# State space columns of a two-block transformer kernel computed in f32 ahead of the shift vector, with the first merge turned to tokens

## Chip, cores and metric

The kernel runs on one core of one Trainium2 chip, as one launch for the whole network. The metric is the device time of one execution in microseconds; the runs shown are three executions on the chip. "PE" is the matmul engine (TensorE), "PEld" its weight load, "DVE" VectorE, "ACT" ScalarE, "POOL" GpSimd, "SP" the engine that issues most DMAs.

## What is computed

Two blocks on 256 tokens of width 2048, batch 1, all in float32. The change touches the first block and the conditioning ahead of it:

```python
mod = silu(c) @ w_ada + b_ada                 # w_ada 2048 x 12288
sh1, sc1, g1, sh2, sc2, g2 = split(mod, 6)
h = rms_norm(x, norm_mix_g) * (1.0 + sc1) + sh1
proj = h @ w_in                               # w_in 2048 x 8192
u, q, k, v, ga, gb = split(proj, ...)         # widths 1024 x4, 2048 x2
y_ssm = s5_branch(u, ...)                     # 64 groups of 16 channels, 64 states
y_att = moba_attention(q, k, v, rel_bias)     # 256 tokens are one block: causal, with a bias
merged = (sigmoid(ga) * (y_ssm @ w_proj_ssm) + sigmoid(gb) * (y_att @ w_proj_attn))
x = x + g1 * (merged @ w_out)
h2 = rms_norm(x, norm_mlp_g) * (1.0 + sc2) + sh2
x = x + g2 * (square(relu(h2 @ w_ff1)) @ w_ff2)
```

The second block (another attention, a recurrence, and an expert layer whose rows are gathered by index) follows; the change edits nothing in it.

## The kernel before

Activations lie on chip transposed: channel on the partition, 256 tokens along the row, so a 2048-wide tensor is 16 chunks of 128 x 256. Weights stream from DRAM in pieces of 1 MB (four chunks of 128 rows, 512 columns). `gemm` (L528) takes one piece at a time. `piece` splits it into a high part (ACT, tile `wh`) and a rest (DVE, tile `wl`), both in the fast fp32r type; the activations are split likewise when they are written (class `HL`). A piece then costs three passes: high times high, high times rest, rest times high. There are two kinds. In kind "A" the weight chunk is the stationary operand and 256 token columns move, so that the output `ga` comes out by channel: 16 matmuls of 256 columns per pass. In kind "B" the tokens are stationary and 512 weight columns move; the output `gb` comes out by token: 8 matmuls of 512 columns per pass.

Order. While the flag `pinned` is set (the prologue), PE, DVE and ACT keep the order in which the program names their work. After that the scheduler of the tile framework places instructions by its own estimates. Between pieces `bg` (called at the end of each part of a piece) hands out credits: `dve` of them let background generators go on (the state space scan, attention, bias set-up), `rate` of them let the stream of conditioning loads go on (`stream`, the later columns of w_ada). TUNE["d1"] is the first of the two in block 1, TUNE["r1"] the second. A `drain` runs a generator to its end, and `need` forces the stream on until a vector is there.

Buffers. 1 MB tiles come from three rings: W with four buffers, H and L with two each. In the prologue all eight serve as landing buffers for the loads (`rot_tile`), in a gemm W holds raw pieces and H and L the split ones.

Prologue, three parts:

- The scale vector (1 + sc1). Sixteen loads of 1 MB of w_ada go through PE with the conditioning vector as stationary operand (tile `aw`, output `adap`; `ada_pe` L261). Beside them `x_in` (L885) transposes x (PE, tile `xt`), copies it to `xT` (DVE) and computes 1/rms of each token (`rstd`); `ssm_prep` (L614) discretizes the state space parameters (transposed in tile `ptp`, copied to `prm`), builds a table of powers of the recurrence (`ssm_table`, L691, tile `tab`: doubling steps of six DVE operations and four small ones each), and the block-diagonal operands (`ssm_blocks`, L722, tiles `bd`, `cd`, transposed on PE as `pb`, `pc`). The state space matrices b_re, b_im are loaded by `load_src` (L315) in runs of 64 bytes into `ssrc`.
- The shift vector sh1, again sixteen loads through PE (loop L921). In the gaps DVE scales x^T by 1/rms and by the scale (`mod_scale`), one chunk per load.
- `mod_shift` adds the shift and splits h into its two fp32r parts, `h1h` and `h1l`.

Main part of block 1, all by `gemm`: u (L953), then q, k, v, gb with a tanh for the sigmoid, w_proj_attn, ga, w_glu, w_proj_ssm with the merge (`ev_mrg`, L1070), w_out. u, q, k, ga, gb, w_glu, w_proj_attn and w_proj_ssm are kind "A", v and w_out kind "B". The scan on u (`ssm`, L761) and attention run as background work.

Of the kernel before, what the change touches and what calls it, by code (L numbers as in the profile page):

```python
# [79 lines left out]
def tile_kernel(ctx: ExitStack, tc: tile.TileContext, I, out):  # L80
# [354 lines left out]

    def modulate(xp, rstd, a, sh, hl, keep=None, then=None):
        n, ts, lag = 2 * len(xp), {}, 3
        for i in range(n + lag):
            if i < n:
                ts[i] = scr([P, L], "mt") if keep is None else keep[i // 8][:, i % 8, :]  # L440
                mod_scale(xp, rstd, a, i, ts[i])
            c = i - lag
            if c >= 0:
                mod_shift(ts[c], sh, c, hl)
                if c in (3, 7) and then is not None:
                    then()
# [167 lines left out]
    def ssm_prep():  # L614
# [268 lines left out]
    r0 = []  # L883

    def x_in():  # L885
        st = tiny([P, 2], "xst")
# [11 lines left out]
        r = rsqrt_of(st, 1.0 / D, 2)
        yield 1.0
        rs = scr([P, L], "rstd")  # L900
        S.copy(rs, spread([r[:, t:t + 1] for t in range(2)], pmisc([P, L], "rows")))
        r0.append(rs)
        yield 0.1
# [928 lines left out]
```

## Time and profile before

| | us |
|---|---|
| median of 3 runs | 3307.53 (3304.88 to 3307.8) |
| the profiled execution, device time | 3305.08 |
| its span in the trace | 3303.3 |
| PE busy | 2944.7 (89%) |
| DVE busy | 2265.6 (69%) |
| ACT busy | 951.7 (29%) |
| POOL busy | 829.6 (25%) |
| DMA moved | 1068.90 MB, mean 324 GB/s |

The span runs from the first to the last instruction of the profiled execution; the device time of the same execution is 1.8 us longer. Busy shares are means over stages with different limits, so they say little about one stage. The stages are: 0 to 75 us the scale vector, 75 to 115 the shift vector, 115 to 786 the gemms of block 1 up to w_out, 786 to 1500 its feed-forward, 1500 to 3303 the second block.

### The profile page before, as it was taken

The page shows a single profiled execution, that of the slowest core. Times are in us where ns is not written, and L with a number is a line of the kernel's source. Part 1 is how long each engine was busy: PE and PEld are TensorE (multiplying, and loading weights), DVE is VectorE, ACT ScalarE, POOL GpSimd, SP SyncE. Part 2 cuts the span into 40 slices and gives each one's busy share as a digit, 9 for nine tenths or more (in the row PEclk, how much of TensorE's full clock was granted, in tenths as well). Part 3 has the DMA queues.
Part 4 walks back from the last instruction along what each step waited for, and adds up shares of the span by engine and source line. Part 5 has one row for each costly group of instructions (what it writes and reads, how often), then busy time and mean ns, then how long its engine had stood idle before and what let it go on. Part 6 is the DMA issues. An engine that isn't in the chain of part 4 may idle for free.

```text
span 3303.3 us, 39102 instructions
## 1 busy us (share of the span) xinstructions
PE 2944.7 (89%) x15580; PEld 2136.2 (65%) x15580; DVE 2265.6 (69%) x3360; ACT 951.7 (29%) x1271; POOL 829.6 (25%) x540
## 2 busy tenths in 40 slices
PE   5899999999999999999999997979777768777777
PEld 2687889988999888898999886544322223222222
DVE  6688779777789888877776647555655565555542
ACT  1333433444433333345346631111111101111000
POOL 1000000000000000000000005656666666666663
PEclk8899999999999999999999998989999989999999
DMA  9876677877899999985783459999999999999998
GB/s 364 306 238 217 203 238 240 318 275 242 295 332 326 325 336 313 336 282 170 262 275 116 146 178 372 420 418 420 421 422 421 421 422 421 422 421 421 421 421 344
DMA packets 280459, 1068.90 MB, mean 324 GB/s; under 512 B 27380, under 2 KB 35991, under 8 KB 189525
## 3 DMA queue, kind: packets, MB, share of 16 engines
q1 hardware_dynamic: 202306, 524.35, 46.0%
q0 software_dynamic: 74752, 538.26, 39.2%
q10 hardware_dynamic: 3220, 3.81, 0.4%
q8 instruction: 122, 2.00, 0.2%
q14 instruction: 59, 0.48, 0.0%
HBM read 1064.24 MB, written 2.11 MB: 323 GB/s over the span
## 4 chain that ended last, share of the span: by engine, by line
PE 59%; DMA 31%; DVE 6%; issue 2%; ACT 1%; POOL 1%; SPq 0%; ACTq 0%; DVEq 0%; POOLq 0%
PE ga L94 30%; DMA dn<-in_peer_down_dram,eid 26%; PE gb L94 16%; PE pe L94 4%; DMA up<-in_peer_up_dram,eid 3%; DVE dn L94 2%; PE adap L94 2%; DMA aw<-in_w_ada_dram 2%; PE xt L94 1%; DMA aw<-in_ada_w_dram 1%; PE wqp L94 1%; PE o L94 1%; PE yp L94 1%; DVE wl L94 1%; PE bu L94 1%
## 5 line engine op out<-in xcount | busy, mean ns | idle before, releaser
L1698 POOL DMA_INDIRECT dn<-in_peer_down_dram,eid x256 | 517.2, 2020 | 2244.9 <-DVE g L94 1948.7
L94 PE MATMUL pe<-up,cdg 128*128 128x512 f32 x1792 | 824.4, 609 | 254.3 <-DMA up<-in_peer_up_dram,eid 203.6
L94 DVE SCALAR_TENSOR_TENSOR dn<-dn,htok 128x2048 f32<-128x2048 f32 x256 | 585.7, 2290 | 486.7 <-DMA dn<-in_peer_down_dram,eid 486.5
L94 PEld LDWEIGHTS pe<-up,cdg 128*128 128x128 f32 x1792 | 333.3, 193 | 735.7 <-issue 511.8
L94 ACT ACTIVATE wh<-w 128x2048 fp32r<-128x2048 f32 (+1 forms) x284 | 538.9, 1897 | 862.1 <-PE ga L94 476.2
L94 DVE TENSOR_TENSOR wl<-w,wh 128x2048 fp32r<-128x2048 f32 (+1 forms) x284 | 643.3, 2266 | 169.4 <-ACT wh L94 119.8
L1698 POOL DMA_INDIRECT up<-in_peer_up_dram,eid x224 | 260.9, 1165 | 139.2 <-issue 51.5
L94 DVE SCALAR_TENSOR_TENSOR acc<-aw,cT,acc 128x2048 f32<-128x2048 f32 x105 | 246.8, 2350 | 64.4 <-DMA aw<-in_ada_w_dram 46.3
L94 PE MATMUL ga<-h2h,wh 128*128 128x256 f32 x1024 | 249.0, 283 | 0.0
L94 PE MATMUL ga<-h2l,wh 128*128 128x256 f32 x1024 | 248.7, 283 | 0.0
L94 PE MATMUL ga<-h1h,wh 128*128 128x256 f32 x896 | 222.2, 287 | 0.0
L94 PE MATMUL ga<-h1l,wh 128*128 128x256 f32 x896 | 219.3, 284 | 0.0
L94 PE MATMUL gb<-wh,ah 128*128 128x512 f32 x512 | 199.6, 390 | 0.0
L94 PE MATMUL gb<-wh,al 128*128 128x512 f32 x512 | 199.4, 390 | 0.0
L94 PEld LDWEIGHTS ga<-h2h,wh 128*128 128x128 f32 x1024 | 196.5, 192 | 1.9 <-issue 1.7
L94 PEld LDWEIGHTS ga<-h2l,wh 128*128 128x128 f32 x1024 | 196.5, 192 | 0.2
L94 PEld LDWEIGHTS ga<-h1h,wh 128*128 128x128 f32 x896 | 172.0, 192 | 15.5 <-issue 12.1
L94 ACT ACTIVATE cdg<-ca,cf 128x128 f32<-128x128 f32 x224 | 77.0, 393 | 354.7 <-PE pe L94 347.4
L94 PEld LDWEIGHTS ga<-h1l,wh 128*128 128x128 f32 x896 | 172.2, 192 | 1.3 <-issue 1.2
L94 PE MATMUL ga<-h2h,wl 128*128 128x256 f32 x1024 | 134.1, 283 | 0.0
L94 PE MATMUL ga<-h3h,wh 128*128 128x256 f32 x528 | 132.1, 288 | 0.0
L94 PE MATMUL ga<-h3l,wh 128*128 128x256 f32 x528 | 132.0, 288 | 0.0
(437 smaller groups left out, 4287.6 us busy)
## 6 DMA issues: line engine op xcount, KB each, us to landing
w<-in_w_ff_dram SPq DMA_DIRECT2D x128, 1024.0 KB, 6.5
w<-in_w_in_dram SPq DMA_DIRECT2D x100, 1024.0 KB, 5.5
aw<-in_w_ada_dram SPq DMA_DIRECT2D x96, 1024.0 KB, 6.9
aw<-in_ada_w_dram SPq DMA_DIRECT2D x96, 1024.0 KB, 7.0
w<-in_w_out_dram SPq DMA_DIRECT2D x32, 1024.0 KB, 5.2
wq<-in_peer_wq_dram SPq DMA_DIRECT2D x16, 1024.0 KB, 10.2
w<-in_w_proj_attn_dram SPq DMA_DIRECT2D x8, 1024.0 KB, 5.2
w<-in_w_proj_ssm_dram SPq DMA_DIRECT2D x8, 1024.0 KB, 5.2
```

Source lines behind the costliest of these rows:

```text
L94: r = f(*a, **k)
L1698: r = G.indirect_dma_start(out=rows_, out_offset=None, in_=table, in_offset=bass.IndirectOffsetOnAxis(ap=idx, axis=0))
```

## The change

What it does, in the order of the program:

1. `x_in` computes 1/rms first and multiplies it in where x^T is copied from PSUM, so that xT holds the normalized input.
2. b_re and b_im are loaded as two contiguous blocks (tile `raw`, 64 groups x 1024 values) and brought into place by 64 small f32 matmuls against columns of the identity (tile `sb`: `raw` stationary, 32 columns moving) and two ACT copies.
3. The first two of the four tables of powers (`ssm_table(0)`, `ssm_table(1)`) are built in the prologue (before: the first there ahead of the scale vector, two more behind it; the rest by the scan itself); the block-diagonal operands (`ssm_blocks`, now in `ssm_mats`) and the attention bias come behind it as background work.
4. The u columns leave the gemms. While the shift vector loads, u is computed in plain f32 from the input scaled by (1 + sc1) alone: eight 1 MB loads of w_in (tile `wu`), 128 matmuls of 128 x 256 (tile `up`). Of the shift vector's own sixteen loads PE takes four, DVE accumulates the other twelve (`ada_both`, tile `acc`).
5. `u_shift`, ahead of the other loads in the stream: the u columns of w_in are loaded once more (8 MB), the shift vector is multiplied with them on PE (32 columns stationary), and the result is added to uT as a bias per channel. Then the rest of the preparation is drained and the scan started.
6. q is the first gemm (stream rate 1.25 instead of 0.65).
7. gb, w_proj_attn, ga and w_proj_ssm (16, 8, 16 and 8 pieces) become kind "B": gates and merge by token. The merged rows are turned back by 32 transposes on PE (tile `mt`) before they are split for w_out.
8. TUNE["d1"] goes from 3.6 to 4.0.

The diff, cut to its core:

```diff
-TUNE = {"r1": 0.65, "d1": 3.6, ...
+TUNE = {"r1": 0.65, "d1": 4.0, ...
...
+    raw = unit([64, 2, 1024], "raw")
+    for k, n in enumerate(("ssm_b_re", "ssm_b_im")):
+        SY.dma_start(raw[:, k, :], I[n][0].rearrange("g n q -> g (n q)"))
...
-        for k, n in enumerate(("ssm_b_re", "ssm_b_im")):
-            SY.dma_start(src[:, k, :].rearrange("p (t q) -> p t q", t=32),
-                        I[n][0].rearrange("(t g) n q -> (g n) t q", g=2))
...
+        par = ident[0:64, 0:64].rearrange("p (t g) -> p g t", g=2)
+        for k in range(2):
+            ps = pmisc([P, 32, 16], "sb")
+            rv = raw[:, k, :].rearrange("g (n q) -> g n q", q=16)
+            for q in range(16):
+                for g in range(2):
+                    T.matmul(ps[64 * g:64 * g + 64, :, q], rv[:, :, q], par[:, g, :], start=True, stop=True,
+                             skip_group_check=True)
+            S.copy(src[:, k, :], ps.rearrange("p t q -> p (t q)"))
+            yield 0.1
         yield from ssm_table(0)
+        yield from ssm_table(1)
+    def ssm_mats():
         for pp in range(2):
             bc = unit([P, 2, 2, 512], "bct")
             for k in range(2):
                 cp2 = 2 * pp + k
                 bct[cp2] = [bc[:, k, i, :].rearrange("p (r c m) -> p r c m", r=2, c=2) for i in range(2)]
                 yield from ssm_blocks(cp2, src)
-        for cp2 in range(1, 3):
-            yield from ssm_table(cp2)
...
+        r = rsqrt_of(st, 1.0 / D, 2)
+        rs = scr([P, L], "rstd")
+        S.copy(rs, spread([r[:, t:t + 1] for t in range(2)], pmisc([P, L], "rows")))
+        yield 1.0
...
-            V.tensor_copy(xp[c2], pt)
+            V.tensor_mul(xp[c2], pt, rs.unsqueeze(1).to_broadcast([P, 2, L]))
...
+    def ada_both(blk, j, g):
+        dest = const([P, 16], "mod")
+        ps = pacc_([P, 512], "adap")
+        acc = unit([P, D], "acc")
+        for kc in range(NC):
+            wt = rot_tile("aw")
+            SY.dma_start(wt, adaw[blk][kc * P:(kc + 1) * P, j * D:(j + 1) * D])
+            if kc == 0:
+                V.tensor_scalar(acc, wt, ccol[blk][:, 0:1], None, op0=OP.mult)
+            elif kc % 4 < 3:
+                V.scalar_tensor_tensor(acc, wt, ccol[blk][:, kc:kc + 1], acc, op0=OP.mult, op1=OP.add)
+            for l, r in [(crep[:, kc, :], wt)] * (kc % 4 == 3) + [(ones[:, 0:32], acc)] * (kc == NC - 1):
+                for q in range(4):
+                    T.matmul(ps[32 * q:32 * q + 32, :], l, r[:, 512 * q:512 * q + 512], start=(kc == 3),
+                             stop=(r is acc), skip_group_check=True)
+            yield 0.0
+        ada_fin(blk, j, ps, dest, g)
...
+    def u_load(nb, k):
+        wt = rot_tile("wu").rearrange("p (c n) -> p c n", c=4)
+        SY.dma_start(wt, w_in[4 * k * P:(4 * k + 4) * P, nb * 512:nb * 512 + 512]
+                     .rearrange("(c p) n -> p c n", p=P))
+        return wt
+    for i in range(8):
+        nb, k = divmod(i, 4)
+        wt = u_load(nb, k)
+        if k == 0:
+            ups = [pmisc([P, 2, L], "up") for _ in range(2)]
+        for _ in range(2):
+            next(g_sh1)
+            bg(0.5, 0)
+        if i == 7:
+            for _ in g_sh1:
+                pass
+        for kk in range(4):
+            c = 4 * k + kk
+            if nb == 0:
+                xx, a_ = xp[c // 2][:, c % 2, :], mods[(1, 1)][:, c:c + 1]
+                if kk % 2:
+                    S.activation(xx, xx, AF.Copy, scale=a_)
+                else:
+                    V.tensor_scalar(xx, xx, a_, None, op0=OP.mult)
+            for j in range(4):
+                T.matmul(ups[j // 2][:, j % 2, :], wt[:, kk, j * P:(j + 1) * P], xp[c // 2][:, c % 2, :],
+                         start=(c == 0 and j % 2 == 0), stop=(c == NC - 1), skip_group_check=True)
+        if nb == 0 and k == 3:
+            for j in range(2):
+                S.copy(uT[:, 2 * j:2 * j + 2, :], ups[j])
     h = HL(16, "h1")
-    for i, _ in enumerate(ada_pe(1, 0, None, crep, pacc_, True)):
-        if i < NC:
-            mod_scale(xp, rstd, mods[(1, 1)], i, xp[i // 2][:, i % 2, :])
-        bg(2.3, 0)
     pre = []
     for c in range(NC):
         mod_shift(xp[c // 2][:, c % 2, :], mods[(1, 0)], c, h)
         if c in (3, 7):
-            pre.append(piece(I["w_in"][0], c - 3, 4, 0, 512))
+            pre.append(piece(w_in, c - 3, 4, 1024, 512))
+        if c == 3:
+            for j in range(2):
+                S.copy(uT[:, 4 + 2 * j:6 + 2 * j, :], ups[j])
     pinned[0] = False
+    g_mats = start(ssm_mats())
+    start(moba_bias())
+    g_scan = []
+    def u_shift():
+        rep = scr([P, NC, 32], "shrep")
+        V.tensor_copy(rep, mods[(1, 0)].unsqueeze(2).to_broadcast([P, NC, 32]))
+        ps = pmisc([P, 512], "adap")
+        for k in range(8):
+            wt = wp.tile([P, 2, 1024], F32, name=nm("wu"), tag="W")
+            SY.dma_start(wt, w_in[2 * k * P:(2 * k + 2) * P, 0:1024].rearrange("(c p) n -> p c n", p=P))
+            for c in range(2):
+                for q in range(2):
+                    T.matmul(ps[32 * (2 * c + q):32 * (2 * c + q) + 32, :], rep[:, 2 * k + c, :],
+                             wt[:, c, 512 * q:512 * q + 512], start=(k == 0), stop=(k == 7),
+                             skip_group_check=True)
+            yield 0.0
+        ev = scr([P, 512], "adae")
+        S.copy(ev, ps)
+        pt = pmisc([P, 4, P], "adat")
+        for b in range(4):
+            T.transpose(pt[:, b, :], ev[:, 128 * b:128 * b + 128], ident)
+        two = tiny([P, 2, 2, 4], "us")
+        V.tensor_copy(two, pt.rearrange("p b (c q r) -> p c q b r", c=2, q=2)[:, :, :, :, 0])
+        b8 = tiny([P, 8], "ub")
+        V.tensor_add(b8.rearrange("p (q b) -> p q b", q=2), two[:, 0], two[:, 1])
+        for c in range(8):
+            S.activation(uT[:, c, :], uT[:, c, :], AF.Identity, bias=b8[:, c:c + 1])
+        drain(g_ssm, g_mats)
+        g_scan.append(start(ssm()))
+        yield 0.0
...
-    uT = unit([P, 8, L], "uT")
-    for nb in range(2):
-        gemm(w_in, NC, nb * 512, [("A", 512, store_pairs([uT], 4 * nb))], h, rate=TUNE["r1"], dve=TUNE["d1"], pre=pre if nb == 0 else ())
-    drain(g_ssm)
-    g_ssm = start(ssm())
...
-        gemm(w_in, NC, 1024 + nb * 512, [("A", 512, store_pairs([qT], 4 * nb, scale=SCALE))], h, rate=TUNE["r1"], dve=TUNE["d1"])
+        gemm(w_in, NC, 1024 + nb * 512, [("A", 512, store_pairs([qT], 4 * nb, scale=SCALE))], h, rate=1.25,
+             dve=TUNE["d1"], pre=pre if nb == 0 else ())
+        if nb == 0:
+            start(moba_flip())
+    drain(g_us)
...
+    def tanh_rows(dst, nb):
+        def ev(t, b):
+            S.activation(dst[t][:, 512 * nb:512 * nb + 512], b, AF.Tanh, scale=0.5)
+        return ev
+    sgb = [unit([P, D], "sgb") for _ in range(2)]
     for nb in range(4):
-        gemm(w_in, NC, 6144 + nb * 512, [("A", 512, store_pairs(sgb, 4 * nb, AF.Tanh, 0.5))], h, rate=TUNE["r1"], dve=TUNE["d1"])
+        gemm(w_in, NC, 6144 + nb * 512, [("B", 512, tanh_rows(sgb, nb))], h, rate=TUNE["r1"], dve=TUNE["d1"])
...
-        gemm(wpa, 8, nb * 512, [("A", 512, ev_m2)], oh, rate=TUNE["r1"], dve=TUNE["d1"])
-    sga = [unit([P, 8, L], "sga") for _ in range(2)]
...
-        gemm(w_in, NC, 4096 + nb * 512, [("A", 512, store_pairs(sga, 4 * nb, AF.Tanh, 0.5))], h, rate=TUNE["r1"], dve=TUNE["d1"])
+        gemm(w_in, NC, 4096 + nb * 512, [("B", 512, tanh_rows(sga, nb))], h, rate=TUNE["r1"], dve=TUNE["d1"])
...
-        def ev_mrg(i, b, nb=nb):
-            c = 4 * nb + 2 * i
-            m = scr([P, 2, L], "mrg")
-            V.scalar_tensor_tensor(m, sga[c // 8][:, c % 8:c % 8 + 2, :], 1.0, b, op0=OP.add, op1=OP.mult)
-            V.tensor_add(m, m, sgb[c // 8][:, c % 8:c % 8 + 2, :])
-            mh.put2(c, m)
-        gemm(I["w_proj_ssm"][0], 8, nb * 512, [("A", 512, ev_mrg)], yh, rate=TUNE["r1"], dve=TUNE["d1"])
+        def ev_mrg(t, b, nb=nb):
+            sl = slice(512 * nb, 512 * nb + 512)
+            m = sga[t][:, sl]
+            V.scalar_tensor_tensor(m, m, 1.0, b, op0=OP.add, op1=OP.mult)
+            V.tensor_add(m, m, sgb[t][:, sl])
+            if t == 0:
+                return
+            for c in (4 * nb, 4 * nb + 2):
+                pt = pmisc([P, 2, L], "mt")
+                for k in range(2):
+                    for tt in range(2):
+                        T.transpose(pt[:, k, tt * P:(tt + 1) * P], sga[tt][:, (c + k) * P:(c + k + 1) * P], ident)
+                mh.put2(c, pt)
+        gemm(I["w_proj_ssm"][0], 8, nb * 512, [("B", 512, ev_mrg)], yh, rate=TUNE["r1"], dve=TUNE["d1"])
```

In the listings below a row is one instruction (or a run of like ones, the last "x" number) in the order in which its engine gets it: operation, output tile, input tiles, shape. A number behind a name counts allocations and differs between the two kernels.

DVE of the kernel before, around the end of the scale vector (`tab` and `el` the second table, `mod_141` the scale vector, `xT` the input):

```order
L94 TENSOR_SCALAR cd_623<-ssrc_135,ca_81 128x2x64 x4
L94 MEMSET tab_634 128x8 x2
...
L94 COPY el_637<-e_142_648 128x8
L94 TENSOR_TENSOR mod_141<-adat_655,colT_103 128x16
L94 SCALAR_TENSOR_TENSOR mod_141<-mod_141,colT_103 128x16
L94 TENSOR_TENSOR ta_662<-tab_634,el_637 128x8x2
L94 TENSOR_TENSOR tab_634<-tab_634,el_637 128x8x2
```

The same place with the change (`tab_535` the second table, `mod_144` the scale vector, `acc_689` the accumulator of the shift vector):

```order
L94 COPY el_538<-e_131_662 128x8
L94 TENSOR_TENSOR mod_144<-adat_675,colT_103 128x16
L94 SCALAR_TENSOR_TENSOR mod_144<-mod_144,colT_103 128x16
L94 TENSOR_SCALAR acc_689<-aw_690,cT_94 128x2048
L94 SCALAR_TENSOR_TENSOR acc_689<-aw_693,cT_94,acc_689 128x2048
L94 TENSOR_SCALAR xT_142<-xT_142,mod_144 128x256 x2
L94 SCALAR_TENSOR_TENSOR acc_689<-aw_718,cT_94,acc_689 128x2048
L94 TENSOR_SCALAR xT_142<-xT_142,mod_144 128x256 x2
```

Before, the block-diagonal operands stand ahead of the scale vector and nearly all of the second table behind it; now the whole second table stands ahead of it, the operands far behind, and two accumulations of the shift vector come before the first scaled chunk.

PE with the change, where the small matmuls for b_re and b_im stand (`ptp` the parameters, `xt` the transposes of x, `sb` the new matmuls):

```order
L94 MATMUL ptp_294<-ca_81,ws_133 128x32 x5
...
L94 MATMUL xt_301<-ca_81,xtok_86 128x128
L94 MATMUL sb_307<-ca_81,raw_130 64x32 x32
L94 MATMUL xt_341<-ca_81,xtok_85 128x128
...
L94 MATMUL adap_145<-aw_347,crep_96 32x512 x4
L94 MATMUL sb_353<-ca_81,raw_130 64x32 x32
L94 MATMUL xt_387<-ca_81,xtok_85 128x128
```

Before, the transposes `xt` and the loads `adap` follow each other there without the 64 `sb` matmuls; the transposes of x behind them, and the DVE operations that need those, now come after.

PE with the change, at the end of the shift vector (`up` the u columns, `adap_688` the shift vector, `ga_976` the first matmul of q):

```order
L94 MATMUL adap_688<-aw_890,crep_96 32x512 x4
L94 MATMUL adap_688<-acc_689,ones_87 32x512 x4
L94 MATMUL adat_902<-ca_81,adae_900 128x128 x4
L94 MATMUL up_810<-xT_143,wu_885 128x256 x2
...
L94 MATMUL rr_1009<-hot_98,rb_100 8x512
L94 MATMUL pb_1016<-ca_81,bd_995 128x128 x4
L94 MATMUL ga_976<-h1h_924,wh_938 128x256
```

Before, `adat` is followed by the gemm of u; now the gemm of q stands there, behind the last of the 128 f32 matmuls and the first of the operands that left the prologue.

## Rows read from the trace of the kernel before

**Rows 1.** Stages: length, busy us (instructions) of PE, PEld, DVE, ACT, POOL; clock, DMA share, GB/s.

```profile
75.00:115.00 40.00, 28.55 (x153) 6.72 (x153) 35.38 (x161) 7.16 (x13) 0.00 (x0) 0.76 0.98 392
115.00:437.00 322.00, 322.00 (x2347) 271.07 (x2348) 230.90 (x411) 116.37 (x122) 0.00 (x0) 1.00 0.69 226
437.00:575.00 138.00, 137.96 (x1102) 124.27 (x1102) 131.04 (x266) 46.04 (x33) 0.00 (x0) 1.00 0.72 243
575.00:786.00 211.00, 211.00 (x1416) 193.30 (x1416) 163.71 (x117) 99.01 (x103) 0.00 (x0) 1.00 0.82 288
786.00:1500.00 714.00, 708.56 (x4635) 645.70 (x4634) 587.86 (x421) 287.11 (x235) 0.00 (x0) 1.00 0.89 310
```

**Rows 2.** Timeline of PE, first gemm of block 1: start, length, operation, last number the records.

```profile
114.88 0.58 PE L94 MATMUL ga<-h1h,wh 128*128 128x256 f32 x1
116.33 0.35 PE L94 MATMUL ga<-h1h,wh 128*128 128x256 f32 x1
```

**Rows 3.** Timeline of PE in the feed-forward: last pass of two pieces of each kind.

```profile
805.06 2.08 PE L94 MATMUL ga<-h2h,wl 128*128 128x256 f32 x16
810.82 2.08 PE L94 MATMUL ga<-h2h,wl 128*128 128x256 f32 x16
...
1083.25 1.98 PE L94 MATMUL gb<-wl,ah 128*128 128x512 f32 x8
1088.69 1.98 PE L94 MATMUL gb<-wl,ah 128*128 128x512 f32 x8
```

**Rows 4.** Timeline of PE: one conditioning load, a run of transposes, a run of f32 matmuls.

```profile
165.57 1.06 PE L94 MATMUL adap<-aw,crep 128*32 128x512 f32 x8
...
1992.85 1.91 PE L94 MATMUL tok<-ca,hf 128*128 128x128 f32 x16
1994.60 13.98 PE L94 MATMUL wqp<-hf,wq 128*128 128x256 f32 x64
```

**Rows 5.** Timeline of DVE in the prologue; in brackets idle time and what ended it.

```profile
34.60 0.30 DVE L94 COPY prm<-ptp 128x160 f32<-128x160 f32 x1
...
36.17 0.08 DVE L94 MEMSET tab<- 128x8 f32 x2
...
38.28 0.69 DVE L94 COPY xT<-xt 128x512 f32<-128x512 f32 x1 [0.65 <-PE xt L94]
38.89 0.17 DVE L94 TENSOR_TENSOR ta<-tab,el 128x16 f32<-128x16 f32 x1
...
40.09 0.67 DVE L94 COPY rrs<-rr 8x512 f32<-8x512 f32 x1
...
41.29 0.17 DVE L94 TENSOR_TENSOR ta<-tab,el 128x32 f32<-128x32 f32 x1
...
42.57 0.16 DVE L94 TENSOR_SCALAR rv<-xst 128x2 f32<-128x2 f32 x1
...
43.67 0.22 DVE L94 TENSOR_TENSOR ta<-tab,el 128x64 f32<-128x64 f32 x1
...
48.84 0.43 DVE L94 TENSOR_TENSOR ta<-tab,el 128x256 f32<-128x256 f32 x1 [1.55 <-PE rows L94]
...
55.90 0.16 DVE L94 COPY el<-e 128x8 f32<-128x8 f32 x1
...
76.33 0.17 DVE L94 TENSOR_TENSOR mod<-adat,colT 128x16 f32<-128x16 f32 x1 [1.26 <-PE adat L94]
```

**Rows 6.** Timeline of PE: transposes of x behind the turned parameters.

```profile
34.37 1.11 PE L94 MATMUL xt<-ca,xtok 128*128 128x128 f32 x4
```

**Rows 7.** Groups of small matmuls: records, busy us, mean ns, idle before.

```profile
L94 PE MATMUL cmp<-cw,blk 128*30 128x128 f32 x128 | 14.3, 273 | 0.0
...
L94 PE MATMUL rms<-ones,sq 128*128 128x1 f32 x64 | 7.4, 245 | 0.0
```

**Rows 8.** Groups of DVE up to 800 us, by shape.

```profile
L94 DVE TENSOR_TENSOR wl<-w,wh 128x2048 fp32r<-128x2048 f32 x101 | 231.2, 2290 | 91.4 <-ACT wh L94 56.1 <-PE ga L94 21.0 <-issue 8.0
L94 DVE SCALAR_TENSOR_TENSOR acc<-aw,cT,acc 128x2048 f32<-128x2048 f32 x25 | 58.7, 2349 | 6.4 <-DMA aw<-in_w_ada_dram 6.3
```

More of the change, by code (lines that the diff above doesn't have):

```diff
@@ L73 @@
 NU = 14
-TUNE = {"r1": 0.65, "d1": 3.6, "pe": "24", "r2": 0.84, "d2": 3.0, "rg": 0.5, "dq": 5.2, "dk": 4.0, "dr": 2.6, "dx": 3.9,
+TUNE = {"r1": 0.65, "d1": 4.0, "pe": "24", "r2": 0.84, "d2": 3.0, "rg": 0.5, "dq": 5.2, "dk": 4.0, "dr": 2.6, "dx": 3.9,
         "do": 5.0, "ro": 0.0, "nf": 3, "tail": 2}
@@ L434, in mod_shift @@
                                op0=OP.add, op1=OP.subtract)
[L436 to L446, printed above, removed]
     def gate_rows(dst, c_):
@@ L882, in tile_kernel @@
     xp = pairs_of(xT)
-    r0 = []
     def x_in():
@@ L895, in x_in @@
                                 xtok[t][:, (2 * c2 + k) * P:(2 * c2 + k + 1) * P], ident)
-            V.tensor_copy(xp[c2], pt)
+            V.tensor_mul(xp[c2], pt, rs.unsqueeze(1).to_broadcast([P, 2, L]))
             yield 0.6
[L898 to L903, printed above, removed]
+    w_in = I["w_in"][0]
     g_x = start(x_in())
@@ L908, in tile_kernel @@
     for i, _ in enumerate(g_sc1):
-        if i == 3:
-            load_src()
         if i == 9:
             g_col = start(columns())
-        if i == 6:
-            start(moba_bias())
         if i == NC - 4:
             drain(g_x, g_col)
+            load_src()
         bg(2.5, 0)
-    rstd = r0[0]
-    start(moba_flip())
+    uT = unit([P, 8, L], "uT")
+    def ada_both(blk, j, g):
[15 more added lines that the diff above has]
+        ada_fin(blk, j, ps, dest, g)
+        yield 0.2
@@ new lines, in tile_kernel @@
+    g_sh1 = ada_both(1, 0, None)
+    def u_load(nb, k):
[28 more added lines that the diff above has]
+                S.copy(uT[:, 2 * j:2 * j + 2, :], ups[j])
@@ L941, in need @@
             cred[0] -= step(stream, False)
-    w_in = I["w_in"][0]
+    g_us = u_shift()
+    stream.append(g_us)
     for j, g_ in ((2, None), (4, "norm_mlp_g"), (3, None), (5, None)):
@@ L1019, in tile_kernel @@
     for nb in range(2):
-        gemm(w_in, NC, 1024 + nb * 512, [("A", 512, store_pairs([qT], 4 * nb, scale=SCALE))], h, rate=TUNE["r1"], dve=TUNE["d1"])
+        gemm(w_in, NC, 1024 + nb * 512, [("A", 512, store_pairs([qT], 4 * nb, scale=SCALE))], h, rate=1.25,
[3 more added lines that the diff above has]
+    drain(g_us)
+    g_ssm = g_scan[0]
     for nb in range(2):
@@ L1029, in tile_kernel @@
         g_moba.append(start(moba(4 * nb, 4 * nb + 4), first=True))
-    sgb = [unit([P, 8, L], "sgb") for _ in range(2)]
+    def tanh_rows(dst, nb):
[3 more added lines that the diff above has]
+    sgb = [unit([P, D], "sgb") for _ in range(2)]
     for nb in range(4):
-        gemm(w_in, NC, 6144 + nb * 512, [("A", 512, store_pairs(sgb, 4 * nb, AF.Tanh, 0.5))], h, rate=TUNE["r1"], dve=TUNE["d1"])
+        gemm(w_in, NC, 6144 + nb * 512, [("B", 512, tanh_rows(sgb, nb))], h, rate=TUNE["r1"], dve=TUNE["d1"])
         if nb == 2:
@@ L1040, in tile_kernel, with ev_m2 @@
     for nb in range(4):
-        def ev_m2(i, b, nb=nb):
-            c = 4 * nb + 2 * i
-            d = sgb[c // 8][:, c % 8:c % 8 + 2, :]
+        def ev_m2(t, b, nb=nb):
+            d = sgb[t][:, 512 * nb:512 * nb + 512]
             V.scalar_tensor_tensor(d, d, 1.0, b, op0=OP.add, op1=OP.mult)
-        gemm(wpa, 8, nb * 512, [("A", 512, ev_m2)], oh, rate=TUNE["r1"], dve=TUNE["d1"])
-    sga = [unit([P, 8, L], "sga") for _ in range(2)]
+        gemm(wpa, 8, nb * 512, [("B", 512, ev_m2)], oh, rate=TUNE["r1"], dve=TUNE["d1"])
+    sga = [unit([P, D], "sga") for _ in range(2)]
     for nb in range(4):
-        gemm(w_in, NC, 4096 + nb * 512, [("A", 512, store_pairs(sga, 4 * nb, AF.Tanh, 0.5))], h, rate=TUNE["r1"], dve=TUNE["d1"])
+        gemm(w_in, NC, 4096 + nb * 512, [("B", 512, tanh_rows(sga, nb))], h, rate=TUNE["r1"], dve=TUNE["d1"])
     drain(g_ssm)
```

3 lines of the change are left out of this document (removed).

## The prediction

> **What bounds the kernel now.** I first cut the span into stages and read how busy each engine is in each. In the main part of block 1, from 115 to 786 us, PE is busy without a gap (322.00 of 322.00, 137.96 of 138.00, 211.00 of 211.00) at the full clock [rows 1]: there, only PE's own work counts, and a microsecond taken from PE is a microsecond gained as long as DVE keeps up. DVE has room in the first and last of these stretches (230.90 of 322, 163.71 of 211), but little in the middle one, where it is busy 131.04 of 138 us [rows 1]. The shift vector's stage, 75 to 115, is another matter: DMA is busy 0.98 of the time at 392 GB/s while PE works 28.55 of 40 us at a mean clock of 0.76, and DVE 35.38 [rows 1]. The loads set the pace and PE has time left; the change puts the u columns there. The first gemm starts at 114.88, its first records 0.21 us apart until 116.33, which is the lower clock (1.2 GHz); behind that they come at 0.12 [rows 2]. The feed-forward behind is PE-bound as well, 708.56 of 714 [rows 1], and the second block isn't touched. So the sum has two parts: where the first gemm of block 1 starts, and how much PE work stands between that and w_out's end.
>
> **PE work behind the start.** A piece of kind A takes 5.76 us (805.06 to 810.82), one of kind B 5.44 (1083.25 to 1088.69) [rows 3].
> - Removed: the gemm of u, 8 pieces x 5.76 = 46.1. Turned from A to B: 16 + 8 + 16 + 8 = 48 pieces x 0.32 = 15.4.
> - Added by `u_shift`: 8 loads at 1.06 each, as a conditioning load costs beside a gemm [rows 4], 8.5; four transposes, 0.5.
> - Added by the merge: 32 transposes of 128 x 128. Sixteen took 1.91 us [rows 4], so 0.12 each, 3.8.
> - Moved here out of the prologue: 32 transposes of the block-diagonal operands, 3.8; the attention bias, four f32 matmuls with 512 columns and its small companions. Sixty-four records of 256 columns take 13.98 [rows 4], 0.216 from start to start when the last one's tail is left off; an f32 matmul is two records, so one with 512 columns is 0.87 and four are 3.5; the companions 0.9.
> Net 21.0 - 61.5 = **-40.5**. The gemm's start at the lower clock (about 0.7, from rows 2) also goes, as PE comes straight from other matmuls.
>
> **The prologue.** Here PE and DVE keep the program's order, so a chain can be walked.
> - The parameters are turned and copied at 34.60 as before [rows 5], and PE's transposes of x behind that end near 35.4 [rows 6].
> - Then come the 128 records of `sb` (64 matmuls, two records each) in two halves, with a group of transposes and one conditioning load between. No row shows this shape. The nearest are 128 matmul records at 14.3 us (30 weight columns, 128 moving) and 64 at 7.4 (128 weight columns, one moving): 0.112 and 0.115 a record [rows 7]. Each has one side of 128; `sb` has 64 and 32. By moving columns alone a record would be 32/256 of 0.216, 0.027. I take 0.08, between but nearer to the rows: 5.1 us per half. Ends: 0.027 and 0.19 (a clock still at its lower level), that is -6.8 and +14 on the sum.
> - So PE is at 40.5, with transposes and load at 42.1, after the second half at 47.2, transposes 47.7, and DVE's copy of them at 48.3.
> - Now DVE builds two tables in a row, both ahead of the scale vector. One table before: 36.17 to 56.06 is 19.9 us, less what stood in between: 1.26 (wait and copy ahead of 38.89), 1.20 (40.09 to 41.29), 1.10 (42.57 to 43.67) and the wait of 1.55 ahead of 48.84 [rows 5]. That leaves 14.8; I use 14.7, and 29.4 for two. With another copy of x and the small columns (about 2) DVE comes to the scale vector near 79.8 and has it at 80.1. Before it began it at 76.33 with a wait of 1.26 for PE [rows 5]; this wait goes, DVE itself is late instead.
> - Behind it DVE does two accumulations of the shift vector before the first scaled chunk: one at 2.35 [rows 8], one without a second operand, somewhere from 0 to 2.35, taken as 1.3, and the scaling itself 0.35. The first `up` matmul starts at 84.1.
> - From there PE has 256 records x 0.216 = 55.3; five conditioning loads (four and the closing one of the accumulator) x 1.06 = 5.3; the turning of the shift vector 0.5; the first shifted chunk 0.6; and a start at the lower clock. Rows 2 show 1.45 us of it; with PE idle for long before I take 1.7 (0 to 3). q's gemm starts at 147.5.
> - What lies beside this: 24 loads of 1 MB at 392 GB/s [rows 1] are 64 us, of which eight can be under way before the scale vector is there, as the rings hold eight; 43 us against 63, hidden. DVE's twelve accumulations, 12 x 2.35 = 28, also lie beside PE's 55. If PE needed the full rate of loads, this cover would be gone and each late load cost 2.7.
> So the first gemm starts 147.5 - 114.9 = **32.6** later.
>
> **DVE and the stream behind.** Removed from DVE after the start: eight remainder splits of u at 2.29 [rows 8], 18.3. Added there: the preparation of the operands. TUNE["d1"] lets 11% more background work through per piece; I cost it at nothing, since over 671 us DVE has 145 us of room [rows 1], and say below what it costs if the room lies in the wrong place. `u_shift` takes eight steps of the stream; the higher rate in q (16 pieces x 0.6 = 9.6 steps) gives them back. The 8 MB come on top of q's 16 and other loads, some 18 MB in 58 us, 3.2 us per load against 2.7 at 392 GB/s: hidden, from 0 to 3. For steps that `need` forces ahead of w_out I add 1 (0 to 5); what slips into the feed-forward is the same work on the same engine.
>
> **Sum:** -40.5 - 0.7 + 32.6 + 1.0 = -7.6 against the profiled execution's 3305.08: 3297.5. The median of the runs is 2.45 above that execution, so on the median 3299.9, **3300**.
>
> **The rivals.**
> - A, the same. Small f32 matmuls don't get cheaper below 0.115 a record. For it: both rows of [rows 7] say so although their shapes have little in common. Against: each of them has 128 columns on one side. Then `sb` costs 14.7, not 10.2, +4.5; with q's loads late by up to 3 the time is 3304 to 3307.
>   The Trainium skill, page "TensorE: Matmul & The Clock Gate", section "Wait — 56ns, not 53.3ns?", has a rule of this kind: without hardware decode the sequencer spends about 62 ns on each matmul, however small. Counting weight load and matmul for each record that is an estimate of 15.9 us for `sb`, and 3305.6 in the end; by the 25 ns floor which it gives otherwise, the sum would go down. The trace's 0.112 to 0.115 sides with the first.
> - B, slower. DVE becomes the bound in the gates. From 437 to 575 it is busy 131.04 of 138 [rows 1], a share of 0.95. A kind-B piece is shorter, 5.44 against 5.76; with the same DVE work per piece the share is 0.95 x 5.76/5.44 = 1.005. With 0.4 more background per piece, over some 36 pieces from k to ga, it is over by up to 0.4 x 36 = 14.4, and PE waits for `wl`. It decides as soon as a piece's split and background, 2.29 and 4 on DVE, last longer than PE's 5.44 and its own background. Then -7.6 + 14.4 = +6.8, 3314. For it: the share of 0.95. Against: it is one stretch of three, two split buffers smooth over some 9 us, and the scan starts later by less than the work that left.
> - C, within A's price: u's second read collides with q's pieces. Then `wh` waits for raw pieces in q only, +3.
> - That the early u gains nothing at all (its f32 records, 55.3, against 46.1 of a gemm) is part of the sum: what makes it pay is the shift stage's idle PE, 28.55 of 40 [rows 1], together with the split work that goes.
>
> **How the numbers follow.** About 0.2% (6.6 us) is what a measurement of this kernel can tell from no change. My forecast of 3300 sits just beyond that bound (-0.23%), so half of its neighbourhood counts as the same. Forecast or better 0.48, A with C 0.30, B 0.22. Low end: `sb` at 0.027 (-6.8), no slow start (-1.7), no forced steps (-1), columns cheaper (-2), and 2 more for the tables: 3286. High end: B with A's price, 3314 + 4.5, 3318. Hence faster 0.48, same 0.30, slower 0.22.
>
> **What would show it.** The scale vector near 80, the first `up` near 84, q's first `ga` near 147.5; `sb` 10 us of PE (A: 15); PE busy without a gap from there to w_out's end, which should come near 778 instead of 786 (B: PE idle for `wl` in the gates, DVE busy over 0.97 there); the same length of feed-forward and second block. A first `up` later than 88, or gaps of PE over 5 us in all behind it, would make the forecast wrong.

## The result and the profile after

The changed kernel takes 3326.63 us in the median of five runs (3322.19 to 3326.72) against 3307.53 before: a ratio of 1.0057, 95% interval 1.0046 to 1.0067. It is slower by 19 us; the forecast was 3300, its upper end 3318. The profiled execution has a span of 3324.9 us against 3303.3, 21.6 longer. In the experiments below, one execution of e9 (5863.4 us) and one of e12 (3738.25) are left out of ratios and medians, and one of e4's five, 3326.22, stays in and lifts e4's ratio.

Three marks divide the 21.6. The first gemm of block 1 starts at 154.3 instead of 114.9 (+39.4; forecast +32.6). From there to the first instruction of the feed-forward (tile `xt` from `dgr`) it is 655.5 us, from 154.3 to 809.8, instead of 677.6, from 114.9 to 792.5 (-22.1; forecast -41.2, and +1 for the stream). From there to the end it is 2515.1 instead of 2510.8 (+4.3; forecast 0). In the twelve executions of the experiments this last part lies between 2510.5 and 2514.0, though none of them edits it; 2515.1 is 1.1 above that, and what it comes from stays open.

Stages of the kernel after, columns as in [rows 1]; the second and third are as long as there, the fourth reaches to `xt`, and the fifth starts there, some 6 us later in the program than the last of [rows 1]:

```profile
86.00:154.00 68.00, 65.15 (x303) 51.27 (x304) 31.54 (x32) 6.80 (x12) 0.00 (x0) 0.97 0.83 305
154.00:476.00 322.00, 322.00 (x1900) 241.49 (x1901) 249.59 (x534) 123.95 (x145) 1.71 (x2) 1.00 0.67 229
476.00:614.00 138.00, 138.00 (x621) 90.75 (x620) 122.06 (x264) 39.82 (x27) 0.00 (x0) 1.00 0.67 229
614.00:810.00 196.00, 190.16 (x964) 158.35 (x961) 140.55 (x109) 89.17 (x101) 0.00 (x0) 0.99 0.79 279
810.00:1524.00 714.00, 712.58 (x4645) 648.47 (x4646) 606.64 (x423) 287.52 (x231) 0.00 (x0) 1.00 0.93 323
```

PE is still busy without a gap through the gemms, at the full clock, and DVE is busy 249.59 of 322 and 122.06 of 138 (before 230.90 and 131.04): not the bound (rival B). So PE has more work there than the sum gave it. The waits of PE from 154 to 810 are 4.5 us at `xt`, as before, and 1.3 at one eviction.

The prologue after, on PE (start, length, operation, records; in brackets idle time before):

```profile
36.89 1.11 PE L94 MATMUL xt<-ca,xtok 128*128 128x128 f32 x4
37.93 3.91 PE L94 MATMUL sb<-ca,raw 64*64 64x32 f32 x64
41.77 1.11 PE L94 MATMUL xt<-ca,xtok 128*128 128x128 f32 x4
42.82 1.94 PE L94 MATMUL adap<-aw,crep 128*32 128x512 f32 x8
44.68 3.96 PE L94 MATMUL sb<-ca,raw 64*64 64x32 f32 x64
...
85.98 9.48 PE L94 MATMUL up<-xT,wu 128*128 128x256 f32 x32 [13.71 <-DVE xT L94]
95.39 1.07 PE L94 MATMUL adap<-aw,crep 128*32 128x512 f32 x8
96.39 7.17 PE L94 MATMUL up<-xT,wu 128*128 128x256 f32 x32
105.65 7.17 PE L94 MATMUL up<-xT,wu 128*128 128x256 f32 x32 [2.09 <-DVE xT L94]
```

and on DVE:

```profile
81.70 0.17 DVE L94 TENSOR_TENSOR mod<-adat,colT 128x16 f32<-128x16 f32 x1
81.90 0.17 DVE L94 SCALAR_TENSOR_TENSOR mod<-mod,colT 128x16 f32<-128x16 f32 x1
82.00 1.28 DVE L94 TENSOR_SCALAR acc<-aw,cT 128x2048 f32<-128x2048 f32 x1
83.31 2.35 DVE L94 SCALAR_TENSOR_TENSOR acc<-aw,cT,acc 128x2048 f32<-128x2048 f32 x1
85.58 0.61 DVE L94 TENSOR_SCALAR xT<-xT,mod 128x256 f32<-128x256 f32 x2
...
100.59 4.74 DVE L94 SCALAR_TENSOR_TENSOR acc<-aw,cT,acc 128x2048 f32<-128x2048 f32 x2 [11.62 <-DMA aw<-in_w_ada_dram]
105.25 0.61 DVE L94 TENSOR_SCALAR xT<-xT,mod 128x256 f32<-128x256 f32 x2
```

The chain is the one of the prediction: parameters, `sb`, transposes, two tables (the wait for PE ahead of the scale vector is gone, DVE itself is late), scale vector at 81.7, two accumulations, first `up` at 86.0. Behind it stands a wait that the prediction did not have: the accumulation at 100.59 waits 11.62 us for its load, the scaling of the next chunks is queued behind it on DVE, and PE is idle 2.09 us for those chunks.

Where the extra PE work in the gemms comes from shows at a single conditioning load. Before, on PE, one load in a gemm of kind A:

```profile
457.85 0.28 PE L94 MATMUL ga<-h1l,wh 128*128 128x256 f32 x1
458.06 1.06 PE L94 MATMUL adap<-aw,crep 128*32 128x512 f32 x8
459.05 0.38 PE L94 MATMUL ga<-h1h,wh 128*128 128x256 f32 x1
459.27 0.28 PE L94 MATMUL ga<-h1l,wh 128*128 128x256 f32 x1
```

After, in a gemm of kind B, two parts of a load:

```profile
453.71 0.39 PE L94 MATMUL gb<-wh,h1l 128*128 128x512 f32 x1
454.03 1.05 PE L94 MATMUL adap<-aw,crep 128*32 128x512 f32 x2
455.00 2.11 PE L94 MATMUL gb<-wl,h1h 128*128 128x512 f32 x8
457.05 1.06 PE L94 MATMUL adap<-aw,crep 128*32 128x512 f32 x6
458.04 0.50 PE L94 MATMUL gb<-wh,h1h 128*128 128x512 f32 x1
458.37 0.39 PE L94 MATMUL gb<-wh,h1l 128*128 128x512 f32 x1
```

A load is four f32 matmuls (eight records) with 32 stationary columns each, into four quarters of the output's partitions. Whole, they hold PE 0.99 us (458.06 to 459.05). Here one matmul (two records) holds it 0.97 us (454.03 to 455.00), and three hold it 0.99. So four take as long as one, as if they ran side by side, and a load that is cut in two costs twice. Call a run of such records with no other PE instruction between them a part. All 54 parts of loads in the gemms of block 1 after say the same: the median part holds PE 0.98 us with one matmul (11 parts) or two (9), 0.99 with three (5) and 1.00 with four (29). Each trip out of the gemm costs besides, beyond the pitch, which is the usual distance of two gemm records: 0.09 on the way out (0.32 from 453.71 to 454.03 where the pitch is 0.23) and 0.10 on the way back (0.33 from 458.04 to 458.37); in kind A the same, 0.09 and 0.10.

Counting the whole stretch from the first gemm to `xt` this way, each record charged with the time to the next start, so that the rows add up to the stretch:

| PE, us | before | after | difference |
|---|---|---|---|
| gemm records x pitch (0.12 kind A, 0.2267 kind B) | 568.3 | 506.9 | -61.4 |
| beyond the pitch; trips out and back | 20.6; 84 | 28.1; 116 | +7.4 |
| loads (`adap`); parts | 35.5; 36 | 52.4; 54 | +16.9 |
| scan's input (`bu`); parts | 16.6; 14 | 20.8; 18 | +4.2 |
| everything else on PE | 36.5 | 47.3 | +10.8 |

The removal is as forecast to 0.1 us. What was added is 39.4, not 21.0. Of the 7.4 beyond the pitch, 32 trips more at 0.19 are 6.1.

The cuts stand in the scheduler's order, where they can be read without a chip. PE of the changed kernel, one load (in the trace its two parts stand at 508.42 and 515.66):

```
L94 MATMUL adap_3543<-aw_4061,crep_96 32x512
L94 MATMUL gb_3914<-wl_3973,ohh_3680 128x512 x3
...
L94 MATMUL adap_3543<-aw_4061,crep_96 32x512 x3
```

The expectations of e1, e2, e4, e5 and e8 below name 39, 46, 43, 64 and 34 parts of loads ahead of their runs, and the traces have 40, 49, 43, 66 and 34. Which part of the change makes the scheduler cut more loads stays open: the higher rate of the stream in q and TUNE["d1"] were not varied alone.

### The profile page after: what moved, and what is told of

It reads as the page before. It is cut to its first block, busy times and chain, and to the rows that moved or that the text cites. A ratio compares the mean times of both kernels' runs of the same rounds, so it can differ in the third digit from the quotient of the medians.

```text
span 3324.9 us, 36857 instructions
## 1 busy us (share of the span) xinstructions
PE 2958.5 (89%) x14440; PEld 2086.5 (63%) x14440; DVE 2266.6 (68%) x3359; ACT 941.0 (28%) x1280; POOL 824.5 (25%) x540
## 4 chain that ended last, share of the span: by engine, by line
PE 62%; DMA 27%; DVE 6%; issue 3%; POOL 1%; ACT 1%; SPq 0%; DVEq 0%; POOLq 0%; ACTq 0%
PE gb L94 26%; DMA dn<-in_peer_down_dram,eid 24%; PE ga L94 20%; PE pe L94 5%; DMA up<-in_peer_up_dram,eid 3%; PE adap L94 2%; DVE dn L94 2%; PE up L94 2%; PE xt L94 1%; PE bu L94 1%; PE yp L94 1%; PE o L94 1%; POOL dn L1789 1%; PE wqp L94 1%; PE sc L94 0%
## 5 line engine op out<-in xcount | busy, mean ns | idle before, releaser
L1789 POOL DMA_INDIRECT dn<-in_peer_down_dram,eid x256 | 508.4, 1986 | 2148.6 <-DVE g L94 1861.7
L94 ACT ACTIVATE wh<-w 128x2048 fp32r<-128x2048 f32 x276 | 523.7, 1897 | 844.0 <-PE gb L94 398.1
L94 DVE TENSOR_TENSOR wl<-w,wh 128x2048 fp32r<-128x2048 f32 x276 | 624.3, 2263 | 152.5 <-ACT wh L94 128.7
L94 DVE SCALAR_TENSOR_TENSOR acc<-aw,cT,acc 128x2048 f32<-128x2048 f32 x116 | 272.5, 2350 | 104.6 <-DMA aw<-in_ada_w_dram 54.0
L94 PEld LDWEIGHTS ga<-h2h,wl 128*128 128x128 f32 x1024 | 127.5, 192 | 0.8 <-DVE al L94 0.8
L94 PE MATMUL gb<-wl,ah 128*128 128x512 f32 x512 | 128.0, 390 | 0.0
L94 PE MATMUL gb<-wh,h1h 128*128 128x512 f32 x320 | 127.8, 400 | 0.0
L94 PE MATMUL gb<-wh,h1l 128*128 128x512 f32 x320 | 126.2, 394 | 0.0
```

What stands on the lines that cost most here:

```text
L94: r = f(*a, **k)
L1789: r = G.indirect_dma_start(out=rows_, out_offset=None, in_=table, in_offset=bass.IndirectOffsetOnAxis(ap=idx, axis=0))
```

## The experiments

**The two halves of the change alone.** Token merges on the kernel before (two of the four gemms are shown; ga and w_proj_ssm go likewise):

```diff
-        gemm(w_in, NC, 6144 + nb * 512, [("A", 512, store_pairs(sgb, 4 * nb, AF.Tanh, 0.5))], h, rate=TUNE["r1"], dve=TUNE["d1"])
+        gemm(w_in, NC, 6144 + nb * 512, [("B", 512, tanh_rows(sgb, nb))], h, rate=TUNE["r1"], dve=TUNE["d1"])
...
-        gemm(wpa, 8, nb * 512, [("A", 512, ev_m2)], oh, rate=TUNE["r1"], dve=TUNE["d1"])
+        gemm(wpa, 8, nb * 512, [("B", 512, ev_m2)], oh, rate=TUNE["r1"], dve=TUNE["d1"])
...
```

> The kernel before with part 7 of the change alone: gb, w_proj_attn, ga and w_proj_ssm by kind B, the merge by token, TUNE d1 left at 3.6; the u columns stay in the gemm. The forecast's own terms give 48 pieces x 0.32 = 15.4 off and 32 transposes = 3.8 on, so -11.6 us (3296). Theory P (parts): the scheduler cuts conditioning loads and scan matmuls in two between the passes of a gemm, each part costs PE about 1 us however few of its records are in it, and each trip out of a gemm and back 0.2 us more; here the PE rows show 39 parts of loads against 36 and 17 parts of bu against 14, and 8 more trips: +7, so about -5 us (3302.5). Rival B of the prediction (DVE bound in the gates) would give no gain, 0 to +5, with PE idle for wl.

3303.38 us, ratio 0.9989 (0.9980 to 0.9999): 3.4 less than the before of its runs (3306.81). In the stretch from the first gemm to `xt` the gemms' pitch gives 15.3, as the forecast had it; the 32 transposes take 3.0 back and other small work 0.8; loads and `bu` come in more parts (40 and 17) and cost 4.2 more; time beyond the pitch grows by 4.7 (92 trips instead of 84, and one wait of 0.9). That leaves 2.6. The forecast's -11.6 had neither the parts nor the trips.

> The changed kernel with part 7 taken back: gates and merge by channel, kind A; the early u, its shift, the two tables and d1 4.0 stay. The forecast's terms for what is left: start +32.6, gemm of u -46.8, shift and moved work +17.2, stream +1: +4 us (3311.5). With the start that the trace of the changed kernel shows (39.4 later instead of 32.6): +11. Theory P adds 46 parts of loads against 36 (eight of them the new loads) and 19 of bu against 14, some 7 us, and 24 trips x 0.2 = 5: about +20 us (3328), as slow as the whole change or slower. If instead the token merges are what loses, this run is near +4.

3321.2 us, 1.0045 (1.0031 to 1.0058): 14.4 slower than the before of its runs. The first gemm starts at 154.5 and PE has 653.0 us from there, with 49 parts of loads and 108 trips. So the early u is what loses, and the token merges on top of it bring no gain: 3321 and 3327, with intervals that overlap. For this run the lines of e1 are taken back in the changed kernel.

**Order on DVE.** The scaling of a chunk is written ahead of the two loads instead of behind:

```diff
+        for kk in range(4 if nb == 0 else 0):
+            c = 4 * k + kk
+            xx, a_ = xp[c // 2][:, c % 2, :], mods[(1, 1)][:, c:c + 1]
+            if kk % 2:
+                S.activation(xx, xx, AF.Copy, scale=a_)
+            else:
+                V.tensor_scalar(xx, xx, a_, None, op0=OP.mult)
         for _ in range(2):
             next(g_sh1)
...
-            if nb == 0:
-                xx, a_ = xp[c // 2][:, c % 2, :], mods[(1, 1)][:, c:c + 1]
...
```

> The changed kernel with the scaling of a group of four input chunks written ahead of the two loads of the shift vector instead of behind them: in DVE's order the scaled chunks come before the accumulations. Both theories: the first up matmul comes 3.6 us earlier (82.4 instead of 86.0) and the wait of 2.1 us for xT at 103.5 goes, where an accumulation waits for its load: -3.6 to -5.7 us, 3321 to 3323, if PE sets the pace of this stage from there on. If the loads set it (24 MB at 392 GB/s are 64 us), the first gemm starts no earlier than before and the time stays at 3326.

3318.06 us, 1.0034 (1.0021 to 1.0048), 8.6 below the change. PE, first matmuls of u:

```profile
82.26 9.35 PE L94 MATMUL up<-xT,wu 128*128 128x256 f32 x32 [10.24 <-DVE xT L94]
91.55 1.06 PE L94 MATMUL adap<-aw,crep 128*32 128x512 f32 x8
92.54 14.08 PE L94 MATMUL up<-xT,wu 128*128 128x256 f32 x64
```

The first `up` is at 82.3 and the wait between the two groups of 32 is gone; the first gemm starts at 148.1, 6.2 earlier. PE sets the pace here, not the loads. The further 2.4 us do not come from the gemms (655.8 us against 655.5 in the change); the last part is 4.3 shorter than in the change's one trace, and the runs of either kernel spread by 3 to 5 us.

**Parts.** An edge in the schedule holds the four matmuls of a load together (the line with `glue = 5` also stands in `u_shift`):

```diff
-                if pinned[0]:
+                if pinned[0] or self.glue > 0:
                     tc.keep_in_program_order(r)
+                self.glue = max(0, self.glue - 1)
...
+            T.glue = 5
             for q in range(4):
                 T.matmul(ps[32 * q:32 * q + 32, :], crep[:, kc, :], wt[:, 512 * q:512 * q + 512],
```

> The changed kernel with a scheduling edge that keeps the four matmuls of a conditioning load (and the next PE instruction) in the order of the program, all else the same. In the PE rows the loads then come in 43 parts instead of 53 for 40 loads; bu goes from 18 to 22 parts. Theory P: 10 x 0.9 = 9 us less for the loads, up to 4 more for bu: -5 us (3321.5). Rival: parts cost what their records cost (0.125 each) and the new work simply is longer: 0.

3316.06 us, 1.0034 (1.0021 to 1.0048), 10.6 below the change. The stretch from the first gemm to `xt` is 646.8 instead of 655.5 with every matmul kept; loads take 42.5 us in 43 parts instead of 52.4 in 54. The reverse, on the kernel before, doubles the parts (`late` is emptied at the next call of `bg`, `half` issues the matmuls named):

```diff
-            for q in range(4):
-                T.matmul(ps[32 * q:32 * q + 32, :], crep[:, kc, :], wt[:, 512 * q:512 * q + 512],
...
+            half((0, 1))
+            late.append(lambda half=half: half((2, 3)))
```

> The kernel before with one edit: of the four matmuls of each conditioning load that goes through PE behind the prologue, the last two are issued a quarter of a piece later, so that every one of the 32 loads stands on PE in two parts (64 parts in the PE rows instead of 36, 27 more trips out of a gemm and back; the same number of matmuls). Theory P: a part of two matmuls takes PE as long as one of four, about 0.98 us, and a trip 0.18: 28 x 0.98 + 27 x 0.18 = +32 us (3339). Rival: a part costs what its records cost, 0.125 each: 27 x 0.18 = +5 (3312).

3337.7 us, 1.0093 (1.0078 to 1.0109): +31.3, where theory P said +32. The stretch from the first gemm to `xt` is 31.6 longer: 26.0 in the loads, which stand in 66 parts instead of 36, and 6.3 beyond the pitch, with 111 trips instead of 84; the longest wait of PE in it, `xt` aside, is 0.5. PE:

```profile
135.57 1.05 PE L94 MATMUL adap<-aw,crep 128*32 128x512 f32 x4
136.55 0.38 PE L94 MATMUL ga<-h1h,wh 128*128 128x256 f32 x1
...
138.65 1.05 PE L94 MATMUL adap<-aw,crep 128*32 128x512 f32 x4
139.64 2.18 PE L94 MATMUL ga<-h1h,wl 128*128 128x256 f32 x16
```

Two matmuls hold PE 0.98 (135.57 to 136.55), the other two again 0.99.

**The second table.**

```diff
         yield from ssm_table(0)
-        yield from ssm_table(1)
...
     def ssm_mats():
+        yield from ssm_table(1)
```

> The changed kernel with the second table of powers built behind the prologue (first thing of the background work) instead of ahead of the scale vector. The prediction's step says that a table costs DVE 14.7 us on the path there: the scale vector then waits for PE and the loads instead, near 75 as in the kernel before, the first up matmul near 79.5 instead of 86.0, so -6 (3320), as long as DVE has the room for the 14.7 us in block 1. If the loads set the pace behind the scale vector, the first gemm starts where it does now and only the room is used up: 0 to +5.

3318.09 us, 1.0038 (1.0024 to 1.0051), 8.5 below the change. The scale vector is there at 67.2, 14.5 earlier and even 9 earlier than in the kernel before, the first `up` at 71.5; the first gemm starts at 146.5, 7.8 earlier. I had expected it no earlier than 75, where the kernel before has it; with b_re and b_im as contiguous rows the last of the sixteen loads starts on PE at 60.5 (61.4 in the change, 70.5 in the kernel before). That the runs of 64 bytes are what held them was not isolated: the run meant for it (e10, below) meets another limit first.

**All together.** Both edits, and the matmuls of loads and of `bu` held together:

> The changed kernel with three edits together: scaling ahead of the accumulations (-8.6 measured alone), the second table behind (-6 expected alone), the matmuls of a load kept together (-10.6 measured alone) and those of the scan's bu kept together too (19 parts instead of the 22 that the second edit made, -2). If they add up: 3326.6 - 27 = 3299, below the kernel before by 7. If the first two remove the same wait (the loads then set the pace): 3305.

3313.19 us, 1.0021 (1.0012 to 1.0030), 14 more than the sum that was expected. The trace has a new wait. PE:

```profile
152.87 1.93 PE L95 MATMUL adap<-wu,shrep 128*32 128x512 f32 x8 [10.75 <-issue]
```

The first matmul of the shift of u stands in PE's order ahead of gemm work and needs `shrep`, the shift vector spread over 32 columns. DVE copies that at 152.3: the scheduler has put the 0.42 us copy behind the second table, which is now background work. So the copy goes into the prologue:

```diff
+    rep = scr([P, NC, 32], "shrep")
+    V.tensor_copy(rep, mods[(1, 0)].unsqueeze(2).to_broadcast([P, NC, 32]))
     pinned[0] = False
```

> As e7, with the copy that spreads the shift vector over 32 columns written as the last step of the prologue. In e7 the scheduler put that copy behind the second table on DVE, and PE stood idle for 10.8 us ahead of the first matmul of the shift of u. Expected: the wait goes, -10.8 us: 3302.5, with the first gemm near 134.5. If the wait belongs to the loads of w_in, it stays: 3313.

3299.21 us, 0.9978 (0.9968 to 0.9988), 14.0 below e7 and 6.8 below the kernel before of its runs (3305.97). The wait is gone, the first gemm at 135.7, `xt` at 783.7, 648.0 behind it.

**The kernel before with parts of the change.** Token merges, and matmuls held together:

> The kernel before with the token merges alone (3303.4 measured) and the matmuls of a load and of bu kept together: 34 parts of loads instead of 39, bu 17 as before, the same trips. Theory P: 5 x 0.98 = -5 us: 3298.5, 8 us below the kernel before. Rival: no change, 3303.

3301.44 us, 0.9984 (0.9975 to 0.9993); against e1 (3303.38) -2, where -5 was expected, and the two intervals overlap. Loads fall from 40 parts to 34 and from 37.9 to 33.7 us, as expected; `yp` of the scan rises from 20.0 to 22.1.

> The kernel before with part 2 of the change alone: b_re and b_im loaded as contiguous rows and brought into place by 64 f32 matmuls on PE (3.9 us a half in the changed kernel). In e6 and e7, where DVE does not hold it up, the scale vector is ready at 66 to 67 us instead of 76, and the prologue of the kernel before waits for its loads (DMA 0.98 busy). If the loads in runs of 64 bytes are what took the 9 us: the first gemm starts near 106 to 108 instead of 114.9, -7 to -9 us (3298 to 3299.5). If the early end in e6 and e7 comes from DVE's order instead, or DVE (33.9 busy of the 41 us from 34 to 75) takes over: 0 to -3.

3320.35 us, 1.0039 (1.0026 to 1.0052): +14, a miss. The `sb` matmuls stand in PE's order ahead of the transposes of x, and DVE, which has the table behind those copies, waits for them twice:

```profile
46.25 0.69 DVE L94 COPY xT<-xt 128x512 f32<-128x512 f32 x1 [4.15 <-PE xt L94]
52.95 0.69 DVE L94 COPY xT<-xt 128x512 f32<-128x512 f32 x1 [6.01 <-PE xt L94]
```

The scale vector comes at 88.8 instead of 76.3 and the first gemm at 129.4. The changed kernel has the same two waits ahead of its tables: its DVE idles 4.19 us before 42.92 and 6.11 before 49.73. So part 2 does not pay by itself.

This trace also has `sb` at both levels of the clock: the first half runs at a granted clock of 0.50 and takes 3.80 us, the second at 0.96 and takes 3.80 as well.

> e8 (token merges, matmuls of a load together, 3301.4) with part 2 of the change as in e10: the two touch different stages and should add up, -7 to -9 on e8: 3293, 13 us below the kernel before. If e10 shows nothing: 3301.

3313.0 us, 1.0023 (1.0014 to 1.0032): e10's loss again, +11.6 on e8.

> e11 with the block-diagonal operands and the two later tables as background work behind the prologue, ahead of the scan (the way of the change). It takes some 20 us of DVE work out of the prologue. If DVE holds up the prologue of e11, up to -5 on e11 (3288); if the loads do, 0; PE has 32 transposes more behind the start, +4, and the scan starts later, which costs nothing as long as it ends before w_glu.

3301.9 us, 0.9988 (0.9979 to 0.9997), 11 below e11, where up to 5 was expected. With the operands out of the prologue the scale vector is at 70.2 and the first gemm at 112.5, 1.2 earlier than in e8; the stretch behind it is 675.2 us instead of 673.6, and the time is e8's.

## Why the prediction was wrong

- **What bounds block 1: right.** PE is busy without a gap behind the first gemm, and DVE never sets the pace (rival B did not come; PE waits for `wl` nowhere in that stretch).
- **The gemm work removed: right**, 61.4 against 61.5.
- **"8 loads at 1.06 each, as a conditioning load costs beside a gemm": the step that failed first.** It took a load for one thing with one price and counted loads, and it put the cutting of `bu` and the trips at nothing. PE pays per part, and the change raises the parts of loads from 36 to 54, of `bu` from 14 to 18 and the trips from 84 to 116. Loads cost 16.9 more instead of 8.5, `bu` 4.2 and the time beyond the pitch 7.4 instead of nothing; the other work that was added or moved cost 10.8, where the sum had 12.5. Together that is 39.4 instead of 21.0, a miss of 18.4. The profiled span missed the forecast by 29.2 in all; 6.8 of it lie in the start (below) and 4.3 in the last part. e4 and e5 show the price from both sides: -8.7 in the stretch of the gemms for 11 parts of loads fewer and four of `bu` more, +31.6 for 30 parts and 27 trips more. The order of PE's instructions has the cuts in it and could be read ahead of the run; I took from it what moved, not what was cut.
  The Trainium skill, page "TensorE: Matmul & The Clock Gate", section "Measured speedup vs the span model", says of matmuls packed into tiles of the array that a group lasts as one matmul and some 4 ns more for each further tile. The rows agree to about 0.01 us (0.97 for one, 0.99 for three and for four). It would have told the price of a cut beforehand.
- **The prologue: right in its chain, short by 6.8 in its end.** The two tables took what was reckoned. The scale vector came at 81.7 instead of 79.8, a small miss made of larger ones: the parameters were turned 2.5 us later (1/rms now stands ahead, and DVE waits 3.53 for a transpose of x before 22.67), and PE was at its lower clock from 38 to 48 us (granted 0.50), so that the load at 42.82 held it 1.86 instead of 1.06 and the transposes beside it 1.05 instead of 0.5. Against that, `sb` took 3.84 and 3.90, 0.060 a record, where the sum had 0.08. That it came near was luck in part. Rival A did not come, and neither did the sum's upper end of 0.19 for a clock at its lower level: the clock was there, and e10 shows the same price at either level.
  Behind the first `up`, 2.1 went to the accumulation that waits for its load ahead of the scaling on DVE, which I had seen in the order and priced only at its own length; 1.0 to a pitch of 0.220 for the f32 records; 0.7 to the start at the lower clock, which cost 2.4 instead of 1.7; and 1.4 to `rr` and `pb` ahead of q, booked behind. The rest came out 0.3 shorter.
  The Trainium skill, page "TensorE: Matmul & The Clock Gate", section "Wait — 56ns, not 53.3ns?", has a rule of about 62 ns per matmul with hardware decode off. The measured 0.060 a record is near it if the records are counted and not the weight loads, as I had counted them. That this rule is the reason is not shown: no run here tells which decode was on, and the weight load was busy without a gap in the same stretch (3.70 of 3.70 us from 38.0 to 41.7).
- **The forecast in two halves was there to be seen.** Its own terms give the early u alone +4 and the token merges -11.6. A gain that rests wholly on the token merges should have raised the chances of the other results; I gave 0.48 to a gain.

Whether the early u can pay at all is not shown. e9 keeps it and gains 6.8 us by three moves of order and one table less on the path, with the same matmuls; but e8, the token merges with loads and `bu` held together and no early u, gains 4.9, and the two intervals overlap.

## What to carry to other kernels

Count the stretches of an engine's order, not only its instructions: the four f32 matmuls of a load held PE 0.99 us together and 0.97 one alone, so a scheduler that cuts such a group in two doubles its price, and each trip between two streams adds 0.19. Where a queue keeps program order, an instruction that waits for a load must not stand ahead of a short one that PE waits for; and when work is moved behind a fence, look which tiny copy the scheduler now puts behind it.

## What was not expected of the hardware

- Four f32 matmuls of 32 stationary and 512 moving columns into four quarters of the partitions held PE 0.99 us, one alone 0.97.
- Leaving the fp32r matmuls of a gemm for f32 ones of loads and coming back cost 0.09 and 0.10 us beyond the pitch, in both kinds of gemm.
- 64 records of f32 with 64 stationary and 32 moving columns took 3.84 us, 0.060 each, at a granted clock of 0.50; in e10 they took 3.80 at 0.50 and 3.80 at 0.96.
